# A gated linear-attention layer on one core: the recurrence in bundles beside the chunks of the weight stream, and the conditioning in two bursts of four pieces instead of three bursts

## The chip, the core and the metric

The kernel runs on one core of a Trainium2 chip. A core has five engines with queues of their own: TensorE (PE, matmuls; PEld is its weight load), VectorE (DVE), ScalarE (ACT), GpSimd (POOL) and SyncE (SP, which here only issues DMAs). The metric is the device time of one execution in microseconds (us); lower is better. Times are medians of several executions; the profile shows one execution.

## The reference

One layer of a decoder trunk runs for two groups that share all weights: a prompt of 256 tokens and eight samples of 8 new tokens (320 token columns in all, model width 2048).

```python
mod = silu(c) @ w_ada + b_ada                      # 2048 -> 6 * 2048, one row per sequence
sh1, sc1, g1, sh2, sc2, g2 = split(mod, 6)
h = rmsnorm(x, norm1_g) * (1 + sc1) + sh1
q, k, v, og, u, ga, gb, alr = split(h @ w_in)      # 2048 -> 11280
loga = log_sigmoid(alr @ w_a2 + b_a) / 16
o, s_new = gla(q / 16, k, v, loga, s0)             # 4 heads: S_t = diag(alpha_t) S_{t-1} + k_t^T v_t ; o_t = q_t S_t
y_a = rmsnorm(o, gla_norm_g) * silu(og)
y_b = pool(u_ext) @ w_pool * pool_scale            # causal means over 2, 4, 8, 16 tokens minus identity
x = x + g1 * ((sigmoid(ga) * y_a + sigmoid(gb) * y_b) @ w_o)
h2 = rmsnorm(x, norm2_g) * (1 + sc2) + sh2
gate, up = split(h2 @ w_gu)
x = x + g2 * ((silu(gate) * up) @ w_down)          # width 5632
```

Outputs are both groups' rows after a last norm, the recurrence's states and the last 15 rows of the pooling branch. All is float32.

## The kernel before

**The weight stream.** Every product of a weight with the tokens is a loop over pieces of 512 KB: `raw_chunk` (L149) loads four K-tiles of 256 columns on SP's queue into one of three raw buffers; `split` makes a rounded part `whi` on ACT (L159) and the rest `wlo` on DVE (L160), 512 columns a time, in five buffers each; `mm3` issues three matmuls of 128 x 128 weights against 320 token columns (L198 to L200). `proj` runs 16 K-tiles in four **chunks** of 24 matmuls for one **unit** of 256 output columns and collects them in one of two `pmain` buffers of PSUM (two banks each); four more banks, `misc`, serve everything else. `evac` copies a unit out (L374, L385, L387, gates from L393 on).

**The stages.** A head stage takes the first slices of the conditioning and of w_in for head 0's units (q, k, v, v, u, og, og, ga, ga, gb, gb) and the gb units of heads 1 and 3. Then w_in runs for heads 1 to 3, unit by unit (9, 11 and 9 units), with the recurrence of the head before and of the same head between their chunks. Then come w_o (`mh`, `ml` are the merged rows), the second norm, and the FFN (w_gu, w_down).

**The conditioning behind the head.** Four of the six sections of w_ada are computed here in 16 **blocks** (`ada_q`) of 512 columns, eight pieces of 512 KB each. `ada_step` does one **burst**: it multiplies its pieces with the conditioning columns in four column groups of PE at once (L250; each float32 matmul stands as two instructions in the trace) and asks for the next `AB` pieces. `ada_pump`, called after each chunk, runs a burst whenever a sum of rates reaches one. A block's last burst is followed by a copy on ACT, one transpose and `ada_out` on DVE. A block takes three bursts, of 3, 3 and 2 pieces.

**The recurrence.** `gla_steps` returns a list of small functions for a head: loads of the states and of w_a2, `s_gk` (gate logits, logarithms on ACT, L764 to L783), `s_exp` for two halves (cumulated sums on PE, L795 and L796, then exponents on ACT), `s_prod` (products with q and k on DVE; its last read of q is L831), `s_vstack`, transposes, `s_attP`, `s_inter` (L959, L963: tokens against states), `s_oback`, `s_state` (L984, L986: states updated and stored), `s_att`, `s_o`, `s_sfin`, a second half with the other four samples, and `s_norm` (L1000 is its matmul). `pool_steps` does the pooling branch; `s_y` multiplies it with w_pool (tile `psy`) and `merge_step` adds both branches. q, k, v, u and og have one buffer each, so the next head's unit can be copied out only when the last reader of the head before is done. Four buffers of tag `w4` hold most of the recurrence's work tiles, and two (tag `S0`) its states.

**The order.** These functions stand in a list, `queue`, and `pump(n)` runs the next n of them. Before each head and after each of its units ten are run; all that are left are run ahead of the first og unit. So a head's whole recurrence is written just behind its u unit. That is the order of the program, and not yet that of the engines: with `schedule_with_timeline_sim=True` the framework places each engine's instructions by their order in the program and by when it expects their operands; instructions given to `keep_in_program_order` keep their order among themselves. DMA issues on SP behind the head are not among those. The trace shows how far this reaches: the states of head 0, asked for behind all of the head stage, are issued at 232.6 us, before that stage ends.

Of the kernel before, what the change touches and what calls it, by code (L numbers as in the profile page):

```python
# [11 lines left out]
F32 = mybir.dt.float32  # L12
# [3 lines left out]
ALU = mybir.AluOpType  # L16
# [4 lines left out]
P = 128  # L21
# [14 lines left out]
PSY = 12  # L36
WB = 5
AB = 3
# [43 lines left out]
def body(tc, A):  # L82
# [119 lines left out]
    def proj(w, col, k0, k1, xh, xl):  # L202

        ps = pmain.tile([P, 2, 512], F32, tag="pm", name=nm("ps"))
        for c0 in range(k0, k1, 4):
            nk = min(4, k1 - c0)
            for j, whi, wlo in split_chunk(w[:, c0:c0 + nk, col:col + 256], nk, 256, (col, c0) if w is win else None):
                kt = c0 + j
                for i in range(2):
                    mm3(ps[:, i, :T], whi[:, i * P:(i + 1) * P], wlo[:, i * P:(i + 1) * P],  # L210
                        xh[kt], xl[kt], kt == k0, kt == k1 - 1)
            ada_pump()
        return ps
# [114 lines left out]
    def s3(ap):  # L328
        return ap.rearrange("p (b t) -> p b t", t=LS)
# [61 lines left out]
    def gates(g, kind, i, src):  # L391
        og, gb = g.og[:, 2 * i:2 * i + 2, :], g.gb[:, 2 * i:2 * i + 2, :]
        if kind == "gb":  # L393
            S.activation(gb, src, AF.Sigmoid)
            return
        sg = gp.tile([P, 2, T], F32, tag="sg", name=nm("sg"))
        S.activation(sg, src, AF.Sigmoid)
# [349 lines left out]
    def gla_steps(g):  # L747
        h = g.h
        st = []
# [58 lines left out]
        def s_prod():  # L808
            EQ, EK, EX, q, k = E["EQ"], E["EK"], E["EX"], g.q, g.k
            for d in range(2):  # L810
                V.tensor_tensor(qeP[:, d, :, 0:LS], s3(EQ[:, d, TP:T]), s3(q[:, d, TP:T]), op=ALU.mult)
                kk = s3(k[:, d, TP:T])
                V.tensor_tensor(keP[:, d, :, 0:LS], s3(EK[:, d, TP:T]), kk, op=ALU.mult)
                V.tensor_copy(E["dec"][:, d], s3(EQ[:, d, TP:T])[:, :, LS - 1])
# [10 lines left out]
            V.tensor_tensor(EQ[:, :, 0:TP], EQ[:, :, 0:TP], q[:, :, 0:TP], op=ALU.mult)  # L825
            V.tensor_tensor(EK[:, :, 0:TP], EK[:, :, 0:TP], k[:, :, 0:TP], op=ALU.mult)
            kq = w4([P, 2, 2, P])
            E["kdA"], E["q2"] = kq[:, 0], kq[:, 1]
            V.tensor_tensor(EX[:, :, 0:P], EX[:, :, 0:P], k[:, :, 0:P], op=ALU.mult)
            V.tensor_tensor(EX[:, :, 144:272], EX[:, :, 144:272], k[:, :, P:TP], op=ALU.mult)  # L830
            V.tensor_tensor(E["q2"], EX[:, :, 272:400], q[:, :, P:TP], op=ALU.mult)  # L831
# [159 lines left out]
        def s_norm():  # L991
# [24 lines left out]
    def pool_steps(g):  # L1016
# [18 lines left out]
        st.append(s_hist)  # L1035
# [16 lines left out]
        st.append(s_buf)  # L1052
# [49 lines left out]
    queue = []  # L1102

    def pump(n):
        for _ in range(min(n, len(queue))):
            queue.pop(0)()

# [4 lines left out]
    def sig0():  # L1112
        for kind in ("og", "ga", "gb"):
            for i in range(2):
                gates(g0, kind, i, getattr(g0, kind)[:, 2 * i:2 * i + 2, :])
        for h in EARLY_GB:
            S.activation(merged[h], merged[h], AF.Sigmoid)
    queue += [sig0] + pst + st[:PSY] + psy + st[PSY:] + [merge_step(g0, E)]
    RATE = 10
    ada_rate(1.0, 36)  # L1120
    for h in range(1, H):
        pump(RATE)
        g = new_group(h)
        for ui, (kind, i, col) in enumerate(units(h)):
# [12 lines left out]
            pump(RATE)  # L1137
        queue += psy + [merge_step(g, E)]
    pump(len(queue))
# [30 lines left out]
    ada_rate(1.4, 36)  # L1170
# [140 lines left out]
    ada_rate(0.75, 48)  # L1311
# [99 lines left out]
```

## Time and profile before

| | |
|---|---|
| median of 3 runs | 1965.23 us (1964.89 to 1965.62) |
| the profiled execution | 1963.95 us, of which 1962.2 are the span from the first to the last instruction |
| mean granted clock of TensorE | 0.997 |
| heads 1 to 3 of w_in, with the recurrence | about 290 to 862 us of the span |
| w_o | about 864 to 990 us |
| FFN | about 998 us to the end |

In the rows below, an instruction's row has its start, its duration, the engine, the line of the kernel, the operation, what it writes and reads, the shape and a count; in brackets stand the idle time of its engine just before and what ended it. A row of windows has the stretch, its length, the busy time of PE, PEld, DVE, ACT and POOL with counts, the granted clock, the busy share of the 16 DMA engines and the rate in GB/s. A row of waits names who waited, for whom, the total, how often and the longest.

### The profile page before, as it was taken

Reading aid. Unit: us, or ns where it says so; the run is one execution under the profiler, and the core shown is the slowest. Engines: PE = TensorE matmul, PEld = TensorE weight load, DVE = VectorE, ACT = ScalarE, POOL = GpSimd, SP = SyncE. Lnnn points to the kernel's source line nnn. Section 1 sums busy time; section 2 is a strip of 40 time slices with the busy share of each in tenths; the row PEclk is TensorE's granted clock in tenths of the full one; section 3 lists DMA queues with packets and bytes.
Section 4 is the critical chain, followed back from the end, with each engine's and each line's share of the span. In section 5 each row is a group of like instructions: output and inputs, shape, how many; then the busy total and the mean of one; then the engine's idle time right before and its main releaser. Section 6 shows DMA issues by size and latency. Waiting matters only on the chain.

```text
span 1962.2 us, 37317 instructions
## 1 busy us (share of the span) xinstructions
PE 1936.7 (99%) x15060; PEld 1850.0 (94%) x15060; DVE 1017.9 (52%) x1909; ACT 826.5 (42%) x1484; POOL 135.9 (7%) x255
## 2 busy tenths in 40 slices
PE   9999999999999999999999999999999999999997
PEld 7899998898999999889999999999999999999997
DVE  3566575575456544674574444444444444444554
ACT  4333374463345433653353333433333434344443
POOL 1012220111011101010020000000000000000000
PEclk9999999999999999999999999999999999999999
DMA  9988645766976786679656666444445444444443
GB/s 321 399 275 268 194 143 180 260 232 205 321 241 209 274 269 217 204 249 323 213 183 196 222 195 193 150 151 144 153 145 153 149 150 150 150 151 146 151 139 102
DMA packets 324607, 400.84 MB, mean 204 GB/s; under 512 B 13545, under 2 KB 264681, under 8 KB 324097
## 3 DMA queue, kind: packets, MB, share of 16 engines
q1 hardware_dynamic: 312082, 357.95, 56.7%
q0 software_dynamic: 12272, 40.25, 5.6%
q8 instruction: 118, 1.93, 0.4%
q14 instruction: 55, 0.45, 0.1%
q10 hardware_dynamic: 80, 0.26, 0.0%
HBM read 373.96 MB, written 24.67 MB: 203 GB/s over the span
## 4 chain that ended last, share of the span: by engine, by line
PE 91%; DMA 1%; DVE 1%; ACT 1%; issue 0%; SPq 0%; DVEq 0%; ACTq 0%
PE ps L198 27%; PE ps L199 27%; PE ps L200 27%; PE pm L250 4%; PE pm L963 1%; PE pm L984 1%; DMA raw<-w_ada 1%; PE pm L132 1%; PE pm L928 1%; DMA raw<-w_o 0%; PE pm L917 0%; PE pm L795 0%; DMA x<-xspill 0%; PE pm L136 0%; PE pm L796 0%
## 5 line engine op out<-in xcount | busy, mean ns | idle before, releaser
L160 DVE TENSOR_TENSOR wlo<-raw,whi 128x512 fp32r<-128x512 f32 x948 | 654.0, 694 | 771.6 <-ACT whi L159 767.8
L159 ACT CAST whi<-raw 128x512 fp32r<-128x512 f32 x948 | 584.6, 621 | 973.3 <-PE ps L199 869.6
L198 PE MATMUL ps<-hh,whi 128*128 128x320 f32 x1408 | 440.7, 313 | 3.0 <-DVE mg L387 1.0
L200 PE MATMUL ps<-hh,wlo 128*128 128x320 f32 x1408 | 438.5, 312 | 0.1
L199 PE MATMUL ps<-hl,whi 128*128 128x320 f32 x1408 | 437.4, 311 | 0.7 <-DVE hl L588 0.7
L198 PE MATMUL ps<-h2h,whi 128*128 128x320 f32 x1408 | 435.8, 310 | 0.0
L199 PE MATMUL ps<-h2l,whi 128*128 128x320 f32 x1408 | 434.9, 309 | 0.8 <-DVE h2l L1261 0.8
L200 PE MATMUL ps<-h2h,wlo 128*128 128x320 f32 x1408 | 434.8, 309 | 0.0
L198 PEld LDWEIGHTS ps<-hh,whi 128*128 128x128 f32 x1408 | 264.3, 188 | 18.8 <-issue 12.0
L199 PEld LDWEIGHTS ps<-hl,whi 128*128 128x128 f32 x1408 | 264.5, 188 | 7.1 <-issue 4.6
L200 PEld LDWEIGHTS ps<-hh,wlo 128*128 128x128 f32 x1408 | 264.4, 188 | 6.2 <-issue 4.9
L198 PEld LDWEIGHTS ps<-h2h,whi 128*128 128x128 f32 x1408 | 264.1, 188 | 2.4 <-issue 2.2
L199 PEld LDWEIGHTS ps<-h2l,whi 128*128 128x128 f32 x1408 | 264.3, 188 | 1.1 <-DVE h2l L1261 1.1
L200 PEld LDWEIGHTS ps<-h2h,wlo 128*128 128x128 f32 x1408 | 264.3, 188 | 0.0
L200 PE MATMUL ps<-ah,wlo 128*128 128x320 f32 x704 | 218.1, 310 | 0.0
L199 PE MATMUL ps<-al,whi 128*128 128x320 f32 x704 | 217.6, 309 | 0.0
L198 PE MATMUL ps<-ah,whi 128*128 128x320 f32 x704 | 217.5, 309 | 0.0
L198 PEld LDWEIGHTS ps<-ah,whi 128*128 128x128 f32 x704 | 132.2, 188 | 0.0
L200 PEld LDWEIGHTS ps<-ah,wlo 128*128 128x128 f32 x704 | 132.2, 188 | 0.0
L199 PEld LDWEIGHTS ps<-al,whi 128*128 128x128 f32 x704 | 132.2, 188 | 0.0
L250 PE MATMUL pm<-raw,scT 128*32 128x128 f32 (+1 forms) x2688 | 99.5, 290 | 1.2 <-DMA raw<-w_ada 1.2
L250 PEld LDWEIGHTS pm<-raw,scT 128*32 128x32 f32 x2688 | 71.0, 109 | 22.1 <-issue 13.4
(328 smaller groups left out, 1574.0 us busy)
## 6 DMA issues: line engine op xcount, KB each, us to landing
raw<-w_ada SPq DMA_DIRECT2D x192, 512.0 KB, 6.3
raw<-w_gu SPq DMA_DIRECT2D x176, 512.0 KB, 3.4
raw<-w_in SPq DMA_DIRECT2D x173, 512.0 KB, 3.9
raw<-w_down SPq DMA_DIRECT2D x79, 512.0 KB, 3.3
S<-state_gla POOLq DMA_DIRECT2D x16, 1024.0 KB, 8.6
o_gs<-S POOLq DMA_DIRECT2D x16, 1024.0 KB, 6.2
raw<-w_o SPq DMA_DIRECT2D x32, 512.0 KB, 5.4
raw<-w_down SPq DMA_DIRECT2D x15, 256.0 KB, 2.5
```

The costliest lines, as they stand in the source:

```text
L132: PE.transpose(out, in_, ident[:k, :k])
L159: S.copy(hi, raw)
L160: V.tensor_sub(lo, raw, hi.bitcast(F32))
L198: PE.matmul(ps, lhsT=whi, rhs=xhi, start=start, stop=False)
L199: PE.matmul(ps, lhsT=whi, rhs=xlo, start=False, stop=False)
L200: PE.matmul(ps, lhsT=wlo, rhs=xhi, start=False, stop=stop)
L250: ins = PE.matmul(ps[32 * j:32 * j + 32, 0:w], lhsT=scT[:, k, :], rhs=raws[j], start=k == 0 if start is None else start, stop=k == KT - 1 ...
L928: PE.matmul(pt, lhsT=E["kdn"][:, s, d * P:(d + 1) * P], rhs=E["vn"][:, s], start=s == 0, stop=s == 1)
L963: PE.matmul(pt[32 * j:32 * j + 32, :], lhsT=qeP[:, d, 4 * gg + j, :], rhs=E["S0", gg, d][:, j], start=False, stop=d == 1, tile_position=(0 ...
L984: PE.matmul(pt, lhsT=kpz[:, j, d * P:(d + 1) * P], rhs=E["vp"][:, gg], start=True, stop=True)
```

## The change

It has four parts. The computation stays the same.

1. Conditioning behind the head: a block of eight pieces takes two bursts of four pieces, with four buffers (`AB`) and rates that are two thirds of those before.
2. The recurrence's steps are grouped into 15 bundles a head instead of 34 steps, and the queue is run by `gla_pump` after each chunk of `proj`, at a rate set for each head: the queue's length over the chunks of 5 units for head 0, and of 8, 10 and 4 units for heads 1 to 3. What is left is still run behind the next u unit.
3. `s_y` makes its two halves one after the other, in one `pmain` buffer each; before, it took both buffers and made them together. The gates of head 0 are split into three functions (gb, og, ga) which are placed behind `s_attP`, ahead of and behind `s_y`, and the sigmoids of the gb units of heads 1 and 3 stand behind head 1's two ga units; all these sigmoids keep the program's order.
4. `s_prod` reads q first, then k.

```diff
-PSY = 12
+PSY = 6
+SPREAD = (8, 10, 4)
-AB = 3
+AB = 4
@@ proj
             ada_pump()
+            gla_pump()
@@ ada_step
-        sec, b = ada_q[n // 3]
-        r = n % 3
+        sec, b = ada_q[n // 2]
+        r = n % 2
-        c0 = 8 * (n // 3) + 3 * r
-        c1 = min(c0 + 3, 8 * (n // 3) + 8)
+        c0 = 4 * n
+        c1 = c0 + 4
...
-                   r == 0 and (c, j) == todo[0], r == 2 and (c, j) == todo[-1])
+                   r == 0 and (c, j) == todo[0], r == 1 and (c, j) == todo[-1])
...
-        if r < 2:
+        if r < 1:
             return
+    queue = []
+    gla_acc = [0.0, 0.0]
+
+    def gla_pump():
+
+        gla_acc[0] += gla_acc[1]
+        while gla_acc[0] >= 1.0:
+            gla_acc[0] -= 1.0
+            if queue:
+                queue.pop(0)()
@@ s_prod
+            kq = w4([P, 2, 2, P])
+            E["kdA"], E["q2"] = kq[:, 0], kq[:, 1]
             for d in range(2):
+                V.tensor_copy(E["dec"][:, d], s3(EQ[:, d, TP:T])[:, :, LS - 1])
                 V.tensor_tensor(qeP[:, d, :, 0:LS], s3(EQ[:, d, TP:T]), s3(q[:, d, TP:T]), op=ALU.mult)
+            V.tensor_tensor(EQ[:, :, 0:TP], EQ[:, :, 0:TP], q[:, :, 0:TP], op=ALU.mult)
+            V.tensor_tensor(E["q2"], EX[:, :, 272:400], q[:, :, P:TP], op=ALU.mult)
+            for d in range(2):
                 kk = s3(k[:, d, TP:T])
                 V.tensor_tensor(keP[:, d, :, 0:LS], s3(EK[:, d, TP:T]), kk, op=ALU.mult)
-                V.tensor_copy(E["dec"][:, d], s3(EQ[:, d, TP:T])[:, :, LS - 1])
...
-            V.tensor_tensor(EQ[:, :, 0:TP], EQ[:, :, 0:TP], q[:, :, 0:TP], op=ALU.mult)
...
-            V.tensor_tensor(E["q2"], EX[:, :, 272:400], q[:, :, P:TP], op=ALU.mult)
@@ gla_steps
-        st += [s_load(0, 0), s_load(0, 1), s_wa2, s_gk, s_exp(0), s_exp(1), s_prod, s_vstack, s_nat2, s_nat3, s_kp(0), s_attP,
-               s_inter(0), s_oback(0)]
-        for d in range(2):
-            st += [s_state(0, d, 0), s_state(0, d, 2), s_load(1, d)]
-        st += [s_att, s_nat, s_kp(1), s_o(0), s_o(1), s_sfin(0), s_sfin(1), s_inter(1), s_oback(1)]
-        for d in range(2):
-            st += [s_state(1, d, 0), s_state(1, d, 2)]
-        st += [s_norm]
+        st += [together(s_load(0, 0), s_load(0, 1), s_wa2), s_gk, together(s_exp(0), s_exp(1)),
+               together(s_prod, s_vstack), together(s_nat2, s_nat3, s_kp(0)), s_attP, s_inter(0),
+               together(s_oback(0), *states(0, 0), s_load(1, 0)), together(*states(0, 1), s_load(1, 1), s_att),
+               together(s_nat, s_kp(1)), together(s_o(0), s_o(1), s_sfin(0), s_sfin(1)), s_inter(1),
+               together(s_oback(1), *states(1, 0)), together(*states(1, 1)), s_norm]
@@ s_y
-            pp = [pmain.tile([P, 2, 512], F32, tag="pm", name=nm("psy")) for _ in range(2)]
-            for k, whi, wlo in split_chunk(A["w_pool"][0, h].rearrange("(k p) n -> p k n", p=P), 2, 512):
-                for e in range(4):
-                    mm3(pp[e // 2][:, e % 2, :T], whi[:, e * P:(e + 1) * P], wlo[:, e * P:(e + 1) * P],
-                        E["dh"][:, k], E["dl"][:, k], k == 0, k == 1)
-            for i, ps in enumerate(pp):
+            parts = list(split_chunk(A["w_pool"][0, h].rearrange("(k p) n -> p k n", p=P), 2, 512))
+            for i in range(2):
+                ps = pmain.tile([P, 2, 512], F32, tag="pm", name=nm("psy"))
+                for k, whi, wlo in parts:
+                    for e in range(2):
+                        c = (2 * i + e) * P
+                        mm3(ps[:, e, :T], whi[:, c:c + P], wlo[:, c:c + P], E["dh"][:, k], E["dl"][:, k],
+                            k == 0, k == 1)
@@ the loop over heads 1 to 3
+    def gla_rate(nunits):
+
+        gla_acc[:] = [0.0, len(queue) / (4.0 * nunits)]
...
-    queue += [sig0] + pst + st[:PSY] + psy + st[PSY:] + [merge_step(g0, E)]
-    RATE = 10
-    ada_rate(1.0, 36)
+    queue += pst + st[:PSY] + [sig0("gb"), sig0("og")] + psy + st[PSY:PSY + 2] + [sig0("ga")]
+    queue += st[PSY + 2:] + [merge_step(g0, E)]
+    ada_rate(2 / 3, 24)
+    gla_rate(5)
     for h in range(1, H):
-        pump(RATE)
         g = new_group(h)
...
             if kind == "og" and i == 0:
-                pump(len(queue))
                 new_gates(g)
             ps = proj(win, col, 0, KT, hh, hl)
             evac(ps, g, kind, i, None)
+            if h == 1 and kind == "ga":
+                tc.keep_in_program_order(S.activation(merged[EARLY_GB[i]], merged[EARLY_GB[i]], AF.Sigmoid))
             if kind == "u":
                 pump(len(queue))
                 st, E = gla_steps(g)
                 pst, psy = pool_steps(g)
                 queue += pst + st
-            pump(RATE)
+                gla_rate(SPREAD[h - 1])
         queue += psy + [merge_step(g, E)]
+    gla_acc[:] = [0.0, 0.0]
     pump(len(queue))
@@ w_o and FFN
-    ada_rate(1.4, 36)
+    ada_rate(0.94, 24)
...
-            while len(ada_done) < 36:
+            while len(ada_done) < 24:
...
-    ada_rate(0.75, 48)
+    ada_rate(0.5, 32)
```

`together` returns a function that calls the functions it was given in turn, and `states(gg, d)` the two `s_state` steps of one half. The pooling branch's `s_hist` and `s_buf` are one step as well.

More of the change, by code (lines that the diff above doesn't have):

```diff
@@ L389, in evac, with gates @@
         gates(g, kind, i, src)
-    def gates(g, kind, i, src):
+    def gates(g, kind, i, src, pin=lambda ins: None):
         og, gb = g.og[:, 2 * i:2 * i + 2, :], g.gb[:, 2 * i:2 * i + 2, :]
         if kind == "gb":
-            S.activation(gb, src, AF.Sigmoid)
+            pin(S.activation(gb, src, AF.Sigmoid))
             return
         sg = gp.tile([P, 2, T], F32, tag="sg", name=nm("sg"))
-        S.activation(sg, src, AF.Sigmoid)
+        pin(S.activation(sg, src, AF.Sigmoid))
         if kind == "og":
@@ L748, in gla_steps @@
         h = g.h
+        pin = tc.keep_in_program_order if h == 0 else lambda ins: None
         st = []
@@ L824, in s_prod @@
                 V.tensor_tensor(kd4[:, :, 2:4, :], kd, kd4[:, :, 0:2, :].bitcast(F32), op=ALU.subtract)
-            V.tensor_tensor(EQ[:, :, 0:TP], EQ[:, :, 0:TP], q[:, :, 0:TP], op=ALU.mult)
             V.tensor_tensor(EK[:, :, 0:TP], EK[:, :, 0:TP], k[:, :, 0:TP], op=ALU.mult)
-            kq = w4([P, 2, 2, P])
-            E["kdA"], E["q2"] = kq[:, 0], kq[:, 1]
             V.tensor_tensor(EX[:, :, 0:P], EX[:, :, 0:P], k[:, :, 0:P], op=ALU.mult)
             V.tensor_tensor(EX[:, :, 144:272], EX[:, :, 144:272], k[:, :, P:TP], op=ALU.mult)
-            V.tensor_tensor(E["q2"], EX[:, :, 272:400], q[:, :, P:TP], op=ALU.mult)
             for d in range(2):
@@ L1005, in s_norm, with together, f, states @@
                 V.scalar_tensor_tensor(o[:, e], o[:, e], GNG[:, e:e + 1], rs, op0=ALU.mult, op1=ALU.mult)
-        st += [s_load(0, 0), s_load(0, 1), s_wa2, s_gk, s_exp(0), s_exp(1), s_prod, s_vstack, s_nat2, s_nat3, s_kp(0), s_attP,
-               s_inter(0), s_oback(0)]
-        for d in range(2):
-            st += [s_state(0, d, 0), s_state(0, d, 2), s_load(1, d)]
-        st += [s_att, s_nat, s_kp(1), s_o(0), s_o(1), s_sfin(0), s_sfin(1), s_inter(1), s_oback(1)]
-        for d in range(2):
-            st += [s_state(1, d, 0), s_state(1, d, 2)]
-        st += [s_norm]
+        def together(*fs):
+            def f():
+                for x in fs:
+                    x()
+            return f
+        def states(gg, d):
+            return s_state(gg, d, 0), s_state(gg, d, 2)
+        st += [together(s_load(0, 0), s_load(0, 1), s_wa2), s_gk, together(s_exp(0), s_exp(1)),
[3 more added lines that the diff above has]
+               together(s_oback(1), *states(1, 0)), together(*states(1, 1)), s_norm]
         return st, E
@@ L1034, in s_hist @@
                 V.tensor_copy(us[:, f, :, 0:PB], pt[:, f * P:f * P + NB * PB].rearrange("p (b r) -> p b r", r=PB))
-        st.append(s_hist)
         def s_buf():
@@ L1051, in s_buf @@
             nc.gpsimd.dma_start(A["o_pp"][0, 0, :, 256 * h:256 * h + 256], t[0:PB, 256:512])
-        st.append(s_buf)
+        st.append(lambda: (s_hist(), s_buf()))
         def s_win():
@@ L1100, in merge_step @@
         return f
-    queue = []
     def pump(n):
@@ L1111, in body, with sig0, f @@
     pst, psy = pool_steps(g0)
-    def sig0():
-        for kind in ("og", "ga", "gb"):
+    def sig0(kind):
+        def f():
             for i in range(2):
-                gates(g0, kind, i, getattr(g0, kind)[:, 2 * i:2 * i + 2, :])
-        for h in EARLY_GB:
-            S.activation(merged[h], merged[h], AF.Sigmoid)
-    queue += [sig0] + pst + st[:PSY] + psy + st[PSY:] + [merge_step(g0, E)]
-    RATE = 10
-    ada_rate(1.0, 36)
+                gates(g0, kind, i, getattr(g0, kind)[:, 2 * i:2 * i + 2, :], tc.keep_in_program_order)
+        return f
+    queue += pst + st[:PSY] + [sig0("gb"), sig0("og")] + psy + st[PSY:PSY + 2] + [sig0("ga")]
+    queue += st[PSY + 2:] + [merge_step(g0, E)]
+    ada_rate(2 / 3, 24)
+    gla_rate(5)
     for h in range(1, H):
-        pump(RATE)
         g = new_group(h)
-        for ui, (kind, i, col) in enumerate(units(h)):
+        for kind, i, col in units(h):
             if kind == "gb" and h in EARLY_GB:
```

## The prediction

> **What bounds the kernel now.** I read the page first, then a table of windows, then PE's waits in the stages that the edit touches, then PE's timeline at each wait and at the conditioning bursts.
>
> ```profile
> span 1962.2 us, 37317 instructions
> PE 1936.7 (99%) x15060; PEld 1850.0 (94%) x15060; DVE 1017.9 (52%) x1909; ACT 826.5 (42%) x1484; POOL 135.9 (7%) x255
> 255.00:875.00 620.00, 615.02 (x5073) 564.69 (x5075) 360.91 (x724) 298.50 (x572) 73.59 (x114) 1.00 0.70 230
> PE psy L198 <- ACT q L385: 2.3, 1, 2.3
> PE pm L796 <- DVE w L783: 1.4, 1, 1.4
> PE pm L250 <- DMA raw<-w_ada: 1.2, 2, 0.7
> PE ps L198 <- ACT mh L335: 0.7, 1, 0.7
> ```
>
> PE is the bound: busy for 99% of the span, and for 615.0 of 620.0 us from 255 to 875 us, where heads 1 to 3 of the weight stream run and the recurrence lies between their chunks. The last four lines are PE's longest waits from 255 to 1000 us on work that the edit moves: 5.6 us together. So the edit can gain in three ways only: PE work that goes away, these waits, and stretches in which PE is busy but slow.
>
> **Conditioning: 16 bursts fewer.** Two of today's bursts on PE:
>
> ```profile
> 528.64 0.31 PE L199 MATMUL ps<-hl,whi 128*128 128x320 f32 x1
> 528.88 1.52 PE L250 MATMUL pm<-raw,scT 128*32 128x128 f32 x48
> 530.33 0.42 PE L200 MATMUL ps<-hh,wlo 128*128 128x320 f32 x1
> 530.58 0.31 PE L198 MATMUL ps<-hh,whi 128*128 128x320 f32 x1
> 530.73 0.31 PE L199 MATMUL ps<-hl,whi 128*128 128x320 f32 x1
> ...
> 546.74 0.31 PE L198 MATMUL ps<-hh,whi 128*128 128x320 f32 x1
> 546.98 1.08 PE L250 MATMUL pm<-raw,scT 128*32 128x128 f32 x32
> 547.99 0.41 PE L199 MATMUL ps<-hl,whi 128*128 128x320 f32 x1
> 548.24 0.31 PE L200 MATMUL ps<-hh,wlo 128*128 128x320 f32 x1
> 548.38 0.31 PE L198 MATMUL ps<-hh,whi 128*128 128x320 f32 x1
> ```
>
> Read the start times. Undisturbed matmuls of the stream start 0.147 us apart (530.58 to 530.73, rounded). From the last one ahead of the x48 burst to the third behind it pass 2.09 us; less three steps of 0.147 the burst costs 1.65. The x32 burst takes 1.64 in the same way, less 0.44: 1.20. So 16 instructions cost 0.45 us, 32 cost 0.89, and about **0.32 us of each burst is fixed**: the way in (0.24 instead of 0.147), the way out, and the second matmul behind it (0.25 instead of 0.147). A block of eight pieces is now x48, x48, x32; after the change it is x64, x64. The instructions stay, one fixed part goes. For 16 blocks behind the head that is 16 x 0.32 = **-5.2 us**. It is PE work, which nothing hides, so all of it should show. Bounds: -4.5, if bursts that lie against recurrence work save less; -6, if the bursts that are now cut in two or three stay whole.
>
> The pieces are the same 512 KB, but SP gets four in a row instead of three, and the stream's own pieces queue behind them.
>
> ```profile
> 890.00:900.00 10.00, 8.52 (x94) 7.72 (x93) 2.20 (x7) 1.49 (x3) 0.15 (x1) 1.00 1.00 328
> ```
>
> At the full rate of this row (328 GB/s) one piece takes 1.6 us and four take 6.4. Bursts come every six chunks (rate 2/3 over four), 6 x 24 x 0.147 = 21 us, so the four are there in time; a piece of w_in has three raw buffers, 3 x 3.5 = 10.6 us, ahead of it. I cost the loads at nothing; where the queues are full they cost one piece more, 1.6 us a burst (last rival).
>
> **The wait at 308 us.** This is where the recurrence of head 0 meets the stream of head 1:
>
> ```profile
> 305.10 0.39 PE L795 MATMUL pm<-cumr,w 128*128 128x272 f32 x1
> 308.00 0.30 PE L200 MATMUL psy<-dh,wlo 128*128 128x320 f32 x1
> 310.63 0.42 PE L198 MATMUL psy<-dh,whi 128*128 128x320 f32 x1 [2.32 <-ACT q L385]
> 309.42 0.41 DVE L831 TENSOR_TENSOR w<-EX,q 128x256 f32<-128x256 f32 x1
> 309.87 0.70 ACT L385 ACTIVATE q<-ps 128x640 f32<-128x640 f32 x1 [1.11 <-DVE w L831]
> 311.41:314.82 3.41, 3.41 (x16) 3.41 (x15) 3.03 (x13) 1.24 (x2) 0.00 (x0) 0.50 0.14 24
> ```
>
> s_y takes both `pmain` buffers at once; the second still holds head 1's q product. That one is copied out by ACT at 309.87, which waits for DVE L831, the last reader of head 0's q (one buffer). So PE's step is 2.63 us instead of 0.147, a loss of 2.5. Then the granted clock is 0.50 for 3.41 us: half of it, 1.7, is lost too. Together **4.2 us**.
>
> The change attacks it three times. s_y uses one buffer after the other, so it needs only the free one. s_prod reads q first: five short DVE operations instead of about a dozen stand ahead of L831's. And s_y is the twelfth step of the queue (1.15 steps a chunk), behind chunk 11 and no longer behind the first unit. What is late next: head 1's first v unit needs the q buffer after chunk 8. exp is written after chunk 6 and prod after chunk 7; in the rows above exp to the end of the copy took 5.5 us (305.10 to 310.57), against two chunks of 3.5 us. That fits, closely. I take -4.2. Bounds: 0 (the wait is only moved) to -4.2.
>
> [...]
>
> **The other waits.** Head 0's first exponent pass waits 1.4 us (L796 on L783), partly since ACT runs a sigmoid of the gates between its logarithm and the cast that L783 needs:
>
> ```profile
> 263.84 1.12 ACT L778 ACTIVATE w<-w,onet 128x512 f32<-128x512 f32 x2
> 265.50 1.28 ACT L397 ACT_TABLE_LOAD   x1
> 266.79 0.74 ACT L397 ACTIVATE sg<-mg 128x640 f32<-128x640 f32 x1
> 267.94 0.92 ACT L782 CAST w<-w 128x512 fp32r<-128x512 f32 x2
> ```
>
> The sigmoids go behind attP, so 2.0 us of ACT leave this place; half of the wait is taken, **-0.6** (bounds -1.4 and 0). The sigmoids now come in three groups with tables of their own at 1.28 us each; ACT is busy 298.5 of 620 us in the stage, so they cost nothing unless they stand ahead of a weight cast. Bundling is taken at nothing:
>
> ```profile
> 446.42 0.60 PE L132 MATMUL pm<-identr,osn 128*128 128x128 f32 x4
> 446.77 0.93 PE L984 MATMUL pm<-vp,kpz 128*128 128x512 f32 x3
> 447.54 0.30 PE L199 MATMUL ps<-hl,whi 128*128 128x320 f32 x1
> ...
> 450.32 0.39 PE L984 MATMUL pm<-vp,kpz 128*128 128x512 f32 x1
> 450.55 0.30 PE L200 MATMUL ps<-hh,wlo 128*128 128x320 f32 x1
> ```
>
> A state product alone takes 0.23 us to the next start, three in a row 0.77, or 0.26 each. Full-width recurrence work pays no entry like a burst's. Bounds: -2 to +2 for what the new order does to short gaps.
>
> **The last head's tail.** Head 3's steps used to be written all ahead of its four gate units; now 18 steps are spread over 16 chunks, so inter(1) is written after chunk 14 and the norm after chunk 16.
>
> ```profile
> 841.41 1.06 PE L963 MATMUL pm<-S,qeP 128*32 128x512 f32 x8
> 860.01 0.70 PE L1000 MATMUL pm<-acc,cst 128*128 128x320 f32 x2
> 863.96 0.42 PE L198 MATMUL ps<-mh,whi 128*128 128x320 f32 x1
> 876.43 1.18 ACT L335 CAST mh<-mg 128x320 fp32r<-128x320 f32 x3
> 876.94 0.41 PE L198 MATMUL ps<-mh,whi 128*128 128x320 f32 x1 [0.71 <-ACT mh L335]
> 770.89 0.58 ACT L374 COPY u<-ps 128x512 f32<-128x512 f32 x1
> ```
>
> Before, 35.0 us pass from inter(1) (841.41) through the norm to the first cast that depends on it (876.43), and w_o waits 0.7 us. From u's copy (770.89) to w_o's start (863.96) 16 chunks take 5.8 us each, recurrence and s_y included. So after the change inter(1) comes about 11.6 us ahead of w_o, whose first three chunks (10.6 us) do not need head 3: cover 22.2 against 35.0, 12.8 us late. A second w_o unit has its own `pmain` buffer and three more such chunks, 10.6 us; the order of PE is made by readiness (w_o already started at 863.96 ahead of the norm's end). With it the wait is 2.2, 1.5 more than today. I take **+1.0**; bounds -0.7 and +12.
>
> **Sum.** -5.2 - 4.2 - 0.6 + 1.0 = -9.0 us. The profiled execution took 1963.95 us (span 1962.2 and 1.75 around it), 1.28 below the median of 1965.23. So 1955.0 for a run like it, 1956.2 as a median.
>
> **The rivals.**
>
> *Only the bursts.* The q copy is still late, at the v unit instead of at s_y; the close fit above speaks for it, the reordered s_prod against. -9.0 + 4.2 gives 1960.4.
>
> [...]
>
> *More goes.* Also the other waits at w_ada (1.2), at mh (0.7), the rest of L796 (0.8), the +1.0 and up to 1.3 us of bursts and gaps: 5.0 less, 1951.2.
>
> *Slower: the tail of head 3.* If PE's order holds w_o's fourth chunk ahead of the second unit, PE stands idle the 12.8 us, 12.1 more than today in place of my +1.0; and after such a wait 1.7 us of clock: 1956.2 + 11.1 + 1.7 = 1969.0. It decides at 10.0 us of added wait: from there the kernel is slower than before. For it: the shorter cover. Against it: an order made by readiness, which fills such a place where it can foresee it.
>
> *The queues are full at w_o.* DMA's share is 1.00 from 890 to 900 us, where xspill, w_o, w_ada and the states meet. If two bursts there wait for a fourth piece and the states' stores come later, 2 x 1.6 + 1.7 of clock: 1961.1; with the tail's 2.2 behind it about 1963.
>
> **How the numbers follow.** Forecast 0.50; only the bursts 0.20; the clock stays 0.04; more goes 0.10; the tail 0.07; full queues 0.09. About 0.2%, 3.9 us, is what a measurement of this kernel can tell from no change, so faster means below 1961.3. The forecast, the clock, more, and 0.16 of "only the bursts" are faster: 0.80. The rest of that and the queues: 0.13 within. The tail: 0.07 slower. The range 1951.0 to 1963.0 leaves out the tail and part of "more goes". The forecast alone: 1953.5 to 1959.
>
> **What would show it.** Bursts x64 from 255 us on, 32 of them, 2.09 us each. No wait of s_y on q's copy, and no row with a granted clock of 0.50 between 30 and 1950 us. L796 waits under 1 us. The first three w_o chunks in sequence, then PE either in the second unit or idle on mh: the latter over 3 us breaks the forecast, as does a wait of v's first matmul on `ps` buffers, or PE waiting for whi on w_o.

## The result, and the profile after

| | before | after |
|---|---|---|
| median (range) | 1965.06 us (1964.18 to 1965.62, 4 runs) | 1952.07 us (1950.37 to 1954.21, 4 runs) |
| profiled execution, its span | 1963.95, 1962.2 | 1950.37, 1948.6 |
| PE work | 1945.6 | 1938.2 |
| PE idle | 14.9 | 8.7 |
| lost to half clock | 1.7 | 1.7 |

The ratio is 0.9935 (95% interval 0.9918 to 0.9952): 13.0 us less, where 9.0 were forecast. The forecast's 1956.2 is too high by 4.1; the range 1951 to 1963 holds the result.

The last three rows of the table are a ledger that all later readings use. **Idle** is the sum of PE's idle times of over 0.06 us in its timeline. **Half clock** is half of the time in which the granted clock is 0.50 and PE is not idle; the stretch behind PE's last matmul, at the end of every execution, is left out. That half is lost is an estimate from the granted clock: in the kernel before the stream's matmuls start 0.27 us apart at 0.50 (311.77 to 313.11 us) and 0.147 at 1.00, by which 1.5 of 3.41 us are lost where the ledger counts 1.7. **Work** is what is left of the span, with the 10.3 to 10.9 us behind PE's last matmul in it. Of the 13.6 us between the two profiled executions, 7.4 are work (the bursts) and 6.2 are waits. The half-clock stretch at 311 us is gone, but another one stands in the head stage (33.75 us), so the table's row does not change; such a stretch near 33 us is there in ten of the study's fourteen profiles, whatever their edit.

PE's waits of the changed kernel from 255 to 1000 us (who waited, for whom, total, how often, longest), all of them that the view names:

```profile
PE pm L137 <- DVE w L859: 1.2, 1, 1.2
PE ps L200 <- DVE h2l L1291: 0.8, 1, 0.8
PE pm L1280 <- DVE dg L1279: 0.2, 1, 0.2
```

The waits on q's copy (2.3), in the exponents (L796, 1.4, and L795 on ACT L782, 0.8), on w_ada (1.2), on mh (0.7) and on whi (0.6) are gone; the first row, at 802 us, is new.

PE's timeline at one burst of the changed kernel:

```profile
526.45 0.31 PE L201 MATMUL ps<-hh,wlo 128*128 128x320 f32 x1
526.68 1.96 PE L252 MATMUL pm<-raw,scT 128*32 128x128 f32 x64
528.57 0.41 PE L199 MATMUL ps<-hh,whi 128*128 128x320 f32 x1
528.82 0.31 PE L200 MATMUL ps<-hl,whi 128*128 128x320 f32 x1
528.97 0.31 PE L201 MATMUL ps<-hh,wlo 128*128 128x320 f32 x1
```

526.45 to 528.97 less three steps of 0.147 is 2.08 us; 2.09 was forecast. A block is 4.16 instead of 4.50. Of the 32 bursts behind 255 us 29 stand whole like this one; three are cut by other work.

Head 0's recurrence against head 1's stream, in the changed kernel's timeline (DVE's last read of q, ACT's copies of q and k, s_y's first matmul), and the window around it:

```profile
313.74 0.41 DVE L831 TENSOR_TENSOR w<-EX,q 128x256 f32<-128x256 f32 x1
317.71 0.69 ACT L398 ACTIVATE q<-ps 128x640 f32<-128x640 f32 x1
322.35 0.70 ACT L398 ACTIVATE k<-ps 128x640 f32<-128x640 f32 x1
333.08 0.30 PE L199 MATMUL psy<-dh,whi 128*128 128x320 f32 x1
300.00:340.00 40.00, 40.00 (x323) 38.23 (x322) 23.96 (x55) 22.25 (x51) 0.48 (x1) 1.00 0.56 175
```

q is copied later than before (317.71, before 309.87), and yet PE is busy for all of the 40 us at full clock. s_y stands 25 us later than it did, so nobody needs q's `pmain` buffer until the v unit starts behind the k unit. k's product is copied at 322.35, and q's buffer is free at 318.4: about 4 us to spare. The last read of q ends 3.6 us ahead of the copy, so the copy does not wait for it either.

The tail of head 3: inter(1), w_o's first matmul, the norm's matmul, the first cast that depends on the norm, and the first copies of w_o's first two units.

```profile
848.81 1.92 PE L979 MATMUL pm<-S,qeP 128*32 128x512 f32 x16
852.81 0.32 PE L199 MATMUL ps<-mh,whi 128*128 128x320 f32 x1
868.42 0.70 PE L1016 MATMUL pm<-acc,cst 128*128 128x320 f32 x2
877.13 0.46 ACT L348 CAST mh<-mg 128x320 fp32r<-128x320 f32 x1 [1.05 <-DVE mg L1123]
885.04 0.48 DVE L1192 SCALAR_TENSOR_TENSOR x<-ps,mod,x 128x256 f32<-128x256 f32 x1 [0.71 <-PE ps L201]
886.97 0.48 DVE L1192 SCALAR_TENSOR_TENSOR x<-ps,mod,x 128x256 f32<-128x256 f32 x1
```

From w_o's start to the cast pass 24.3 us, more than twice what three chunks take, and PE does not wait for mh. The last two rows show why: the first two units of w_o are copied out 1.9 us apart, where one unit takes 14 us. They ran side by side, and the second unit's three chunks that need no head 3 filled the time.

### The profile page after: what moved, and what is told of

Same layout as the page of the kernel before. It is cut to its first block, busy times and chain, and to the rows that moved or that the text cites. A ratio compares the mean times of both kernels' runs of the same rounds, so it can differ in the third digit from the quotient of the medians.

```text
span 1948.6 us, 37288 instructions
## 1 busy us (share of the span) xinstructions
PE 1929.4 (99%) x15060; PEld 1851.4 (95%) x15060; DVE 1015.9 (52%) x1909; ACT 824.1 (42%) x1482; POOL 135.8 (7%) x255
## 3 DMA queue, kind: packets, MB, share of 16 engines
q8 instruction: 118, 1.93, 0.4%
## 4 chain that ended last, share of the span: by engine, by line
PE 92%; DVE 1%; DMA 1%; ACT 0%; issue 0%; DVEq 0%; ACTq 0%
PE ps L199 28%; PE ps L200 27%; PE ps L201 27%; PE pm L252 4%; PE pm L979 1%; PE pm L1000 1%; PE pm L944 1%; PE pm L133 1%; DMA raw<-w_in 1%; PE pm L933 0%; PE pm L810 0%; PE psy L199 0%; PE pm L137 0%; PE psy L200 0%; PE psy L201 0%
```

## The experiments

All medians are set against the kernel before, run on the same chip; its median was between 1964.7 and 1966.2. In the ledger the span, work, idle and clock are those of the one profiled execution.

| run | median us (range) | ratio (95%) | span | work | idle | clock |
|---|---|---|---|---|---|---|
| e1 before, two bursts | 1964.63 (1960.01 to 1972.5) | 1.000 (0.9988 to 1.0011) | 1967.6 | 1938.3 | 22.9 | 6.4 |
| e2 after, three bursts | 1974.95 (1973.92 to 1978.7) | 1.0055 (1.0043 to 1.0067) | 1972.9 | 1944.3 | 20.8 | 7.8 |
| e3 before, s_y in halves | 1964.48 (1962.07 to 1967.19) | 0.9998 (0.9989 to 1.0006) | 1961.7 | 1945.4 | 14.6 | 1.7 |
| e4 e3 and q first | 1963.9 (1961.24 to 1964.76) | 0.9994 (0.9986 to 1.0003) | 1961.8 | 1945.0 | 13.4 | 3.4 |
| e5 pace and gates only | 1977.06 (1975.55 to 1978.25) | 1.0055 (1.0038 to 1.0072) | 1975.6 | 1945.0 | 22.2 | 8.4 |
| e6 after, old s_y | 1951.73 (1950.92 to 1953.21) | 0.9928 (0.9913 to 0.9943) | 1950.7 | 1936.2 | 11.1 | 3.4 |
| e7 before, second q buffer | 1962.57 (1961.11 to 1967.2) | 0.9986 (0.9977 to 0.9996) | 1960.3 | 1946.2 | 12.4 | 1.7 |
| e8 e2, second q buffer | 1972.42 (1969.99 to 1972.99) | 1.003 (1.0017 to 1.0043) | 1971.2 | 1944.9 | 16.5 | 9.8 |
| e9 e2, head 0 early | 1964.71 (1962.21 to 1970.74) | 1.000 (0.999 to 1.001) | 1968.9 | 1943.2 | 17.7 | 8.0 |
| e10 after, head 0 early | 1950.87 (1948.55 to 1951.58) | 0.9924 (0.9911 to 0.9938) | 1949.8 | 1934.8 | 11.6 | 3.4 |
| e11 two bursts, e4's edits | 1963.2 (1958.09 to 1966.08) | 0.9987 (0.9977 to 0.9998) | 1963.3 | 1940.5 | 16.3 | 6.5 |
| e12 after, single steps | 1952.51 (1951.85 to 1956.11) | 0.9934 (0.992 to 0.9947) | 1954.2 | 1936.4 | 11.0 | 6.8 |

The profiles of e1 and e9 fell 5 and 6 us above their medians (profiled 1969.39 and 1970.74), so their idle and clock are those of a longer execution than most.

**The column "work" answers the first question alone.** The six kernels with two bursts (after, e1, e6, e10, e11, e12) lie between 1934.8 and 1940.5, mean 1937.4; the eight with three (before, e2, e3, e4, e5, e7, e8, e9) between 1943.2 and 1946.2, mean 1945.0. Nothing else in the table sorts them so. The bursts are worth 7.5 us of work in the mean. Between two kernels that differ in the bursts alone it is 7.3 (before, e1), 6.1 (e2, after), 8.4 (e9, e10) and 4.5 (e4, e11), so single profiles scatter by some 2 us. Counted from the start times at the bursts alone (all bursts behind 250 us, with what the matmuls of the stream beside them take over 0.147 us), it is 73.1 us before and 66.8 after: 6.3.

### e1: the bursts alone

The kernel before, with part 1 of the change:

```diff
-AB = 3
+AB = 4
-        sec, b = ada_q[n // 3]
+        sec, b = ada_q[n // 2]
...
-    ada_rate(1.0, 36)
+    ada_rate(2 / 3, 24)
```

> The kernel before with part 1 of the change alone (two bursts of four pieces). Theory (each burst has a fixed price of 0.32 us on PE and nothing else moves): 5.2 us under the kernel before, about 1959.9; the wait of s_y for q's copy near 308 us and the half-clock stretch behind it stay. Rival (the rarer and longer loads also end the waits for w_ada and for w_o's pieces, 1.2 and 0.6 us): about 1958. Rival (longer loads in a row starve the stream): 1962 or more, with waits for whi.

The work fell by 7.3 and the time did not move. PE's waits of e1 from 255 to 1000 us:

```profile
PE pm L795 <- ACT w L782: 3.6, 2, 2.8
PE pm L132 <- ACT osn L970: 3.5, 1, 3.5
PE pm L250 <- DMA raw<-w_ada: 3.0, 2, 2.1
PE ps L198 <- ACT whi L159: 1.9, 2, 1.5
```

The wait on q's copy is not among them, though neither s_y nor s_prod was touched. The last read of q and q's copy in e1:

```profile
301.08 0.42 DVE L831 TENSOR_TENSOR w<-EX,q 128x256 f32<-128x256 f32 x1
312.03 0.70 ACT L385 ACTIVATE q<-ps 128x640 f32<-128x640 f32 x1
```

With fewer bursts the planner has placed head 0's exponents earlier (L804 at 299.55 us instead of 307.15), and q is read for the last time 8 us earlier than in the kernel before (309.42). So the bursts alone end this wait, in the old order. But other waits have come, and two half-clock stretches behind them (274.70 and 373.69 us): the bursts' gain is given back as waits. The theory missed in time and in the wait. The rival with starved loads has the time, and waits on loads did grow (w_ada from 1.2 to 3.0, whi from 0.6 to 1.9), but the two longest waits are not on loads.

### e2: everything but the bursts

The changed kernel, with part 1 undone:

```diff
-AB = 4
+AB = 3
-    ada_rate(2 / 3, 24)
+    ada_rate(1.0, 36)
```

> The changed kernel with part 1 undone (three bursts a block). Theory: the same 5.2 us the other way, about 1957.3. Rival (bursts and pace depend on each other, so that three bursts among the paced steps bring back waits for w_ada): 1959 or more. Rival (the pace alone carries the gain): 1953.

It is 23 us slower than the changed kernel, of which only 6.1 are work. Its longest waits from 255 to 1000 us, and PE's timeline around the first:

```profile
PE ps L199 <- ACT q L398: 7.8, 1, 7.8
PE ps L199 <- ACT mh L348: 2.5, 1, 2.5
PE pm L979 <- DMA S<-state_gla: 1.5, 1, 1.5
PE ps L200 <- DVE ml L349: 1.2, 1, 1.2
```

```profile
303.66 1.13 PE L779 MATMUL pm<-wa,alr 48*128 48x256 f32 x4
...
319.45 1.50 PE L252 MATMUL pm<-raw,scT 128*32 128x128 f32 x44
328.78 0.64 PE L199 MATMUL ps<-hh,whi 128*128 128x320 f32 x1 [7.83 <-ACT q L398]
```

The v unit's first matmul stands for 7.83 us on q's buffer; this is the wait that the prediction named as late next. The gate logits of head 0 (L779) stand at 303.66 us. In the changed kernel they stand at 256.76, as in the kernel before (256.16). The recurrence started 47 us later, so the exponents and q's last reader (L831 at 325.71) came after the place where q's buffer is needed. The theory's 1957.3 missed by 18 us. The rival in which bursts and pace depend on each other is the one that held, but by way of q's copy; the waits on w_ada, which it named, are 0.6 us.

### e3 and e4: s_y in halves, and q first in s_prod, in the old order

The kernel before; e3 has the first edit, e4 both:

```diff
-            pp = [pmain.tile([P, 2, 512], F32, tag="pm", name=nm("psy")) for _ in range(2)]
+            for i in range(2):
+                ps = pmain.tile([P, 2, 512], F32, tag="pm", name=nm("psy"))
...
+            V.tensor_tensor(EQ[:, :, 0:TP], EQ[:, :, 0:TP], q[:, :, 0:TP], op=ALU.mult)
+            V.tensor_tensor(E["q2"], EX[:, :, 272:400], q[:, :, P:TP], op=ALU.mult)
             for d in range(2):
                 kk = s3(k[:, d, TP:T])
```

> The kernel before with the two halves of s_y one after the other in one PSUM buffer each, nothing else. Theory (s_y's wait for a second buffer is the cause at 308 us): the wait of 2.3 us and the half clock go, 4.2 us less, about 1960.9. Rival (the next unit needs the same buffer, so PE waits there for the same copy of q): 1964 to 1965, and a wait for q's copy in another row.

> The kernel before with s_y in halves and with s_prod reading q first. Theory (either ends the wait): as with s_y alone, about 1960.9. Rival (with s_y alone the wait only moves, and q's copy has to come earlier too): 1.5 us below the run with s_y alone at least, as the readers of q are through about 1.5 us earlier.

The wait in e3, then in e4, with DVE's last read of q in e4 (L816 there):

```profile
310.07 0.42 PE L198 MATMUL psy<-dh,whi 128*128 128x320 f32 x1 [2.32 <-ACT q L385]
```

```profile
PE psy L198 <- ACT q L385: 1.9, 1, 1.9
309.13 0.41 DVE L816 TENSOR_TENSOR w<-EX,q 128x256 f32<-128x256 f32 x1
```

s_y in halves leaves the wait as it was, at 307.7 us; reading q first shortens it by 0.4. The half-clock stretch follows in both (1.7 and 3.4 us in the ledger). The two edits that were to end this wait do not, and the rows show why. In e3 the first half's twelve matmuls run from 305.83 to 307.7, and then the second half needs the other `pmain` buffer, which holds q's product as before. In e4 q comes first in the program, but not on DVE: the planner still places products with k ahead of q's last read, which comes only 0.3 us earlier than in the kernel before (309.42). Of the expectations, e3's rival has the time (1964 to 1965) but not the other row; in e4 neither held, with 0.6 us below e3 where the rival asked for 1.5.

### e5 and e6: the order alone, and the change without its new s_y

e5 is the kernel before with parts 2 and the gates of part 3 only; e6 is the changed kernel with the s_y of before, whose edit is:

```diff
-            for i in range(2):
-                ps = pmain.tile([P, 2, 512], F32, tag="pm", name=nm("psy"))
+            pp = [pmain.tile([P, 2, 512], F32, tag="pm", name=nm("psy")) for _ in range(2)]
```

> The kernel before with the pace alone: bundles, steps behind each chunk and the sigmoids in three groups, but three bursts a block, s_y in both buffers and s_prod in its old order. Theory (the pace takes no PE work away; what it does to the waits hangs on where the order puts s_gk of head 0): PE's work without waits and without half clock stays within 1.5 us of the kernel before (1945.6 us of its span). With s_gk ahead of 290 us as in the changed kernel the waits are about 10 us and the time 1957 to 1960; with s_gk near 304 us, as in the changed kernel with three bursts, PE waits some 8 us for q's copy and the time is 1968 to 1976. Rival (the pace carries the gain whatever the rest): 1953 or less.

> The changed kernel with s_y in two buffers at once as before. Theory (s_y's buffers are not what ended the wait at 308 us, its place in the order is): within 3 us of the changed kernel's 1952, with s_gk of head 0 still ahead of 290 us and no wait of PE for q's copy above 1 us. Rival (the single buffer ended it): the wait of s_y is back, 1956 or more.

e5's longest wait:

```profile
PE ps L199 <- ACT k L398: 7.8, 1, 7.8
```

e5 is as slow as e2 and for the same reason: 7.8 us on the copies of L398 (k's and, behind it, q's), with L779 at 304.1 us. That is the theory's second case, 1 us above its range. e6 is as fast as the changed kernel (1951.73 and 1952.07) and has no wait on q, as its theory said. s_y in halves is worth nothing here.

### e7 and e8: a second buffer for q

The kernel before (e7) and e2 (e8), with:

```diff
-        g.q = gp.tile([P, 2, T], F32, tag="q", name=nm("q"))
+        g.q = (lp if h % 2 else gp).tile([P, 2, T], F32, tag="q", name=nm("q"))
```

> The kernel before with a second buffer for q (heads 1 and 3 have their own), so that q's copy waits for no reader of the head before. Theory (the wait at 308 us is for the one buffer of q, and the half clock follows from it): no wait of s_y there and no half clock behind it, 4.2 us less, about 1960.9. Rival (the half clock comes without the wait): 2.5 less, 1962.6. Rival (s_y's second buffer is then held by the next product, or the order moves): 1964 or more.

> The changed kernel with three bursts a block (measured 1974.95) and a second buffer for q. Theory (its loss is the 7.8 us wait for q's copy and the half clock of 10.2 us that goes with it, some 3.9 us lost): 10 to 13 us less than without the second buffer, 1962 to 1965. Rival (its loss is spread, or lies in the bursts among the paced steps): 1970 or more.

In e7 (the kernel before) q of head 1 has a buffer of its own. The wait at 308 us and the half clock at 311 are gone, with 2.9 us of the time against the same chip's 1965.5 (by the interval 0.8 to 4.5). So the chain that the prediction read there was the right one: s_y on `pmain`, `pmain` on the copy, the copy on q's single buffer. The time is nearer the rival's 1962.6 than the theory's 1960.9, but that rival kept the half clock at 311; the profile has a new one at 993.85 us, by the second norm. In e8 (e2 with the edit) q's wait is gone too, but other waits stay or come (2.8 us on a state, 2.5 on mh, 1.5 at L137), the half clock grows from 7.8 to 9.8, and the gain is 2.5 of 23 us: the theory missed, and the rival (1970 or more) held. q's buffer is one place where a late recurrence shows, not the reason.

### e9 and e10: head 0's first steps early

e2 (e9) and the changed kernel (e10), with:

```diff
+    pump(len(pst) + 3)
     gla_rate(5)
     for h in range(1, H):
```

> The changed kernel with three bursts a block (as in e2) and the first steps of head 0 (its pooling steps, loads, s_gk, both s_exp) run ahead of head 1's first unit instead of one a chunk. Computation unchanged. Theory A, place of the gate logits decides: in e2 and e5 head 0's s_gk stands at 304 us and PE waits 7.8 us for q's copy; in the changed kernel it stands at 257. With it early again the wait for q goes (7.8 us and up to 3 us of half clock less), while the work stays that of three bursts (about 1944.5 of PE) and the tail of head 3 keeps its 3 to 6 us of waits: about 1963 to 1966. Theory B, three bursts with this pace are late anyway, since bursts stand between the recurrence's steps wherever it begins: q's wait stays over 3 us and the time stays at 1971 or above.

> The changed kernel with the first steps of head 0 (pooling steps, loads, s_gk, both s_exp) run ahead of head 1's first unit instead of one a chunk. Computation unchanged. Theory A (work is fixed by the bursts, and in the changed kernel s_gk is early already): PE's work stays at 1938 within 2, waits at 7 to 11: 1950 to 1954, no difference to the changed kernel. Theory B (the pace of head 0 still costs): the rest of the steps now comes over fewer queue entries, prod earlier, and 1 to 3 us go: 1948 to 1950.

e9 is e2 with one line more: 1964.71 instead of 1974.95. L779 stands at 258.70 us, L831 at 294.12, and q's wait is gone. What keeps e9 from the changed kernel is 5 us of work and its tail, from its waits between 255 and 1000 us:

```profile
PE pm L979 <- DMA S<-state_gla: 3.9, 1, 3.9
PE ps L199 <- ACT mh L348: 2.5, 1, 2.5
PE pm L133 <- ACT adasb L305: 1.8, 1, 1.8
```

The place of head 0's first steps, with the logits among them, therefore costs about 10 us in e2, as theory A had it. In the changed kernel they are early already, and e10 gains nothing that can be told apart, as its theory A had it (1950.87, its range overlaps that of 1952.07). It is the fastest median of the study all the same.

### e11: the bursts with both small edits, in the old order

The kernel before with e4's edits and e1's, of which the first lines are:

```diff
-AB = 3
+AB = 4
...
-            pp = [pmain.tile([P, 2, 512], F32, tag="pm", name=nm("psy")) for _ in range(2)]
+            for i in range(2):
+                ps = pmain.tile([P, 2, 512], F32, tag="pm", name=nm("psy"))
```

> The kernel before with two bursts of four, s_y in halves and q read first, but its steps still single and run ten at a time (no pace, no bundles, no new place for the gates). Computation unchanged. Theory A, the order made by the pace is what lets the bursts' 6 to 7 us through: PE's work 1938 to 1940, but waits of 10 us or more with half clock as in e1 remain, 1960 to 1966. Theory B, the reordered s_y and s_prod remove the waits once bursts are fewer: waits under 8 us and no half clock in the first head, 1952 to 1956.

1963.2: the work is 5.1 lower than in the kernel before, the time 1.5, as theory A had it. As in e1, q's copy is not waited for (DVE's last read of q runs at 300.75). Its longest waits, and ACT's timeline at the first:

```profile
PE pm L795 <- ACT w L782: 3.6, 2, 2.8
PE ps L198 <- ACT whi L159: 2.3, 2, 2.2
```

```profile
259.00 0.60 ACT L774 ACTIVATE w<-pm 128x512 f32<-128x512 f32 x1 [0.22 <-PE pm L764]
259.62 1.28 ACT L776 ACT_TABLE_LOAD   x1
260.91 0.63 ACT L776 ACTIVATE w<-w 128x512 f32<-128x512 f32 x1
261.56 1.28 ACT L397 ACT_TABLE_LOAD   x1
262.86 0.74 ACT L397 ACTIVATE sg<-og 128x640 f32<-128x640 f32 x1
263.62 1.28 ACT L778 ACT_TABLE_LOAD   x1
264.91 0.72 ACT L778 ACTIVATE w<-w,onet 128x512 f32<-128x512 f32 x1
267.20 0.61 ACT L782 CAST w<-w 128x512 fp32r<-128x512 f32 x1
```

A sigmoid of the gates (L397), with a table of its own, stands in the middle of the logarithm's chain; the cast that PE waits for starts 8.2 us behind L774. A second one does the same at 268 us. In the changed kernel, where part 3 has moved the gates, the same chain has no such guest:

```profile
257.92 0.60 ACT L789 ACTIVATE w<-pm 128x512 f32<-128x512 f32 x1 [1.02 <-PE pm L779]
258.54 1.28 ACT L791 ACT_TABLE_LOAD   x1
259.83 0.63 ACT L791 ACTIVATE w<-w 128x512 f32<-128x512 f32 x1
260.48 1.28 ACT L793 ACT_TABLE_LOAD   x1
261.78 0.72 ACT L793 ACTIVATE w<-w,onet 128x512 f32<-128x512 f32 x1
263.54 0.62 ACT L797 CAST w<-w 128x512 fp32r<-128x512 f32 x1
```

5.6 us from L789 to the cast, and no wait in the exponents. All six kernels with the gates in their old place wait 2.2 to 3.6 us for this cast or for what DVE makes of it (L783), and none of the other eight does in head 0. But the gates were not moved alone: all eight have the new pace as well. Nor is the new place free in every order. In e2 a sigmoid of the gates (L410, with its table from 320.34 to 322.37 us) stands between the exponents that q's last reader needs, while PE waits.

### e12: single steps at the same pace

The changed kernel, with the list of single steps of before:

```diff
-PSY = 6
+PSY = 12
-        st += [together(s_load(0, 0), s_load(0, 1), s_wa2), s_gk, together(s_exp(0), s_exp(1)),
+        st += [s_load(0, 0), s_load(0, 1), s_wa2, s_gk, s_exp(0), s_exp(1), s_prod, s_vstack, s_nat2, s_nat3, s_kp(0), s_attP,
...
```

> The changed kernel with head steps single again (34 steps a head instead of 15 bundles), at the same pace by chunks (the queue's length over the same units, so more steps fall to a chunk). Computation unchanged. Theory A (bundles cost and bring nothing, the pace and the bursts do it): PE's work within 2 of the changed kernel's 1938, s_gk of head 0 at about 257 us, no wait of 2 us or more between 255 and 875 us: 1950 to 1956. Theory B (the placement is so delicate that another cut of the list moves head 0's s_gk or the tail of head 3, as the third burst did): a wait of 2 us or more on q's copy, on a state or on mh, with half clock behind it: 1957 to 1966.

1952.51: no difference from the changed kernel. Bundles bring nothing, as theory A had it; the 1.2 us wait at L137 is not there without them, and two others are (0.8 and 0.7 us in the exponents of later heads). The profiled execution has 13.65 us of half clock in the head stage, far from the edit.

## Why the prediction was right, and where it was not

The likeliest case held in direction and in what goes (fewer bursts, no wait at 308 us). But 1952.07 lies outside the 1953.5 to 1959 that it was given alone, and nearest the rival "more goes" (1951.2, chance 0.10): the waits that this rival listed, on w_ada, at mh and in the exponents, all went.

- **Bursts, -5.2.** (16 x 0.32 is 5.1.) The right term, too small: 7.5 by the means of the two groups, 4.5 to 8.4 by single pairs, 6.3 counted at the bursts themselves. All but the 4.5 are beyond its bound of -6. Whole bursts, as in the timeline above, give 0.34 a block, 5.4 for sixteen; what the rest is made of no run separates.
- **Loads, 0.** Right in the changed kernel, which waits for neither w_ada nor whi; in e1 these two waits are 3.1 us longer than before.
- **The wait at 308 us, -4.2.** The chain was right, and its price fits (e7: 2.9, within 0.8 to 4.5). The cause of its going was wrong, so that it went was partly luck. The prediction named three attacks on it: s_y in halves, q first, and s_y later. e3 and e4 show that the first two do not end it, and e6 that s_y in halves is not needed. The order with its later s_y does not end it alone either: with three bursts the wait is 7.8 us (e2, e5). The wait is gone in all six kernels with two bursts, in the old order (e1, e11, where q is last read 8 us earlier than before) and in the new. Of the eight with three bursts it is gone only with a second buffer (e7, e8) or an early start (e9).
- **What is late next: "That fits, closely."** In the new order it fits with 4 us to spare with two bursts, and misses by 7.8 us with three (e2, e5). The rival "only the bursts" had this mechanism, but priced the wait at 2.5 us.
- **L796, -0.6.** All of the 1.4 went; the rows of e11 and after support the reason given, the sigmoids. The prediction's list of PE's longest waits had left out 0.8 us at L795 on ACT L782, in the same chain, which is more than the 0.7 at mh; it went too.
- **Bundling, 0.** Held (e12).
- **Tail, +1.0.** The second unit did fill PE, as assumed. The estimate that the dependent cast comes 35.0 - 11.6 = 23.4 us behind w_o's start came out at 24.3, but by luck, from other numbers: inter(1) only 4.0 us ahead of w_o, and 28.3 us from there to the cast. Nothing waited, so -0.7 instead of +1.0. The rival's mechanism exists: e2, e8 and e9 stand 2.5 us on mh and 1.2 on ml.
- **The sum.** The step that failed is the sum itself, which adds the parts as if each stood alone. That its total came within 4.1 us rests on the early place of head 0's logits, which the prediction did not look at. Bursts alone give 0, the order alone +12 (e5), both together -14 (e6, with q read first besides). Work adds up, within its scatter of some 2 us; waits belong to one order of the whole. Why the planner puts head 0's logits 47 us later in the new order when a block has three bursts, and its exponents 8 us earlier in the old order when a block has two, stays open: the runs show that it does, what it costs, and that one line brings the logits back.

The chance of 0.04 for "the clock stays" was for a half clock at 311 us that comes without the wait. No run shows that: with the wait gone, the half clock at 311 us went in e7 and in the changed kernel. The sign "no row with a granted clock of 0.50 between 30 and 1950 us" did not hold to the letter: one stretch stands at 33.75 us, ahead of all that the edit moves.

## What to carry to other kernels

Keep two ledgers: work on the bounding engine, which adds up edit by edit, and waits, which have to be read anew for each combination of edits. An edit can also end a wait that it does not touch: fewer bursts ended the one on q's copy. When an edit frees work and the time does not move, look for the waits that came with the new order before giving the edit up. Look first at where the chain that frees a single buffer begins: a start 47 us later cost more here than the buffer itself, and calling its first steps earlier was one line.

## What was not expected of the hardware

In four profiles the starts of half-clock stretches lie, within each, whole steps of **3.413 us** apart. In e2 they begin at 34.01, 324.14, 901.00 and 1006.81 us: the distances are 85, 169 and 31 times 3.4133. In e1 two begin at 274.70 and 373.69 us, 29 steps apart; in the kernel before the stretch at 311.41 and the one at the end (1953.22) are 481 steps apart, in the changed kernel those at 33.75 and 1938.38 are 558. A cell is here one such step, counted from the start of a stretch of the same execution. What goes with half clock in these runs is PE's idle time within the cell just before: in the kernel before 2.32 us (308.00 to 311.41 us, then 0.50 for 3.41 us). Two cells in sequence of e8, then three of e1 (stretch, length, busy PE, PEld, DVE, ACT, POOL, clock, DMA share, GB/s):

```profile
328.00:331.42 3.42, 1.89 (x15) 1.65 (x13) 3.34 (x16) 3.41 (x12) 0.00 (x0) 1.00 0.75 288
331.42:334.83 3.41, 3.41 (x17) 3.41 (x17) 3.41 (x8) 2.19 (x5) 0.00 (x0) 0.50 0.38 114
```

```profile
875.45:878.86 3.41, 2.55 (x18) 2.29 (x16) 3.41 (x8) 2.13 (x5) 0.00 (x0) 1.00 1.03 396
878.86:882.27 3.41, 2.19 (x66) 2.00 (x67) 2.18 (x6) 1.01 (x4) 0.00 (x0) 1.00 0.69 221
882.27:885.69 3.42, 3.42 (x25) 3.41 (x24) 0.65 (x2) 0.82 (x3) 0.00 (x0) 1.00 1.00 354
```

In e8 a wait of 1.53 us lies whole in one cell, and the next cell has a granted clock of 0.50. In e1 a wait of 2.07 us falls into two cells, with 0.86 and 1.22 us of idle, and the clock stays at 1.00. Counted between 60 us and the last 20 us of all fourteen profiles, the full-clock cells with 2.19 us of idle or more were followed by half clock, and so were those of 1.53 and 1.92; of those with 1.50 and less none were (1.37 in the kernel before at 267.03 us and 1.25 in the changed kernel at 801.72 us among them), but for three cells around the second norm with some 0.2 us of idle, which this does not explain. In the head stage of the changed kernel a cell of 1.15 us (30.33 to 33.75) was. One cell of 1.93 (e5) has its half clock only one cell later, where PE stood idle. So, by estimate from these cells, a wait of about 1.5 to 3 us may cost 1.7 us more (half of 3.41, as the ledger counts) or not, by where the cells divide it. That this is behind the spread of kernels with such waits (e1's times lie 12 us apart) was not tried.
